# A one-core hybrid decoder layer: which projection runs beside the SSD, and how many attention heads run beside the SSD's output projection

## The chip, the cores and the metric

The kernel runs on one core of one Trainium2 chip. The metric is the device time of one execution in microseconds (us); the median of three runs is shown. PE is TensorE (matmuls; PEld its weight loads), DVE is VectorE, ACT is ScalarE, POOL is GpSimd, SP is SyncE.

## The reference

One decoder layer over 1024 tokens of width 1024, in float32:

- a mixer: one input projection of the normed input feeds an SSD (a chunked state-space scan, 8 chunks of 128 tokens, 8 heads) and a stick-breaking attention of 8 heads of width 64; both outputs are normed, joined and projected by `w_out`;
- a cross-attention to 256 memory tokens: 4 heads of width 128, with keys and values projected from the normed memory by `w_xk` and `w_xv`;
- an MLP with squared ReLU, 1024 to 4096 and back, and a final norm.

```
y_all = concat([rmsnorm(ssd(...) * silu(z)), rmsnorm(stick_breaking_attention(q, k, v))])
h = x + y_all @ w_out
m = rmsnorm(mem, g_mem);  k = m @ w_xk;  v = m @ w_xv
h = h + softmax(q k^T / sqrt(128)) v @ w_o
h = h + relu(rmsnorm(h) @ w1)^2 @ w2
```

## The kernel before, in words

Every large product is made in three matmuls: each operand is split into a high and a low part (`split`, L170: ACT rounds the high part, DVE subtracts it), and `mm3` (L207 to L210) adds high x high, high x low and low x high. Weights come as pieces of 128 x 512 floats, 256 KB (`piece`, L187): one DMA from SP's queue into a staging buffer (tag `wst`, two buffers, and a third, `wst3`, while the input stage lives), then the split into `whi` and `wlo`, a ring of six each. Pieces carry an earlier priority than the code around them (`later(-EARLY)`).

The order of the work is made in two steps. First, generators write it down: each yields a cost, and `interleave` (L229) runs two of them so that their shares of the given totals advance together. Then a scheduler, which is part of the language, orders each engine's instructions by priority, and the priority is the place at which an instruction was written; one that is ready can go ahead of an earlier one that is not, within the buffers that are free.

The stages around the change are these:

- **SSD** (`ssd`, L513; 8 chunks), interleaved with the fillers of `early`: `proj_z1`, `proj_v(0)`, `proj_qk(0)`, and the first `NF` = 1 of the list `late`. Fillers use four PSUM buffers here (`mm_ps`).
- **Attention** (`attention`, L700), heads 0 to `NHA` - 1, interleaved with the rest of `late`. A head has four steps of cost 3/36, 7/36, 11/36 and 15/36. A step makes scores (`z`, PE), their sigmoid (ACT), a running product along the row (`stay`, the scan of L756 on DVE), transposes (`wT`, PE), a split (ACT, DVE), and products with the values (`ops`, PE). Queries, keys and values go through DRAM (`qd`, `kd`, `vd`): SP stores them, POOL loads them for each head. Fillers use three PSUM buffers here (`qk_ps`).
- **Output projection of the SSD** (`out_first`, L835; total 17.6: 16 blocks of 12 matmuls with 512 columns, tile `o`, and eight transposing steps of 0.2), interleaved with the heads from `NHA` on.
- **Output projection of the attention** (L923 on), which needs all heads: `yB` (the scaled and split heads), 16 blocks in `o`, and a row factor `ro` from the sum of squares `osum`, through `sps` (PE) and one power on POOL.

The fillers: `proj_qk(pr)` (L577) projects the queries and keys of heads 2 pr and 2 pr + 1 from four weight pieces; it yields 2.0 four times, for 24 matmuls of 512 columns each, and each block is split and stored in four (queries) or six (keys) DMAs. `proj_v(ch)` (L567) yields 1.0 eight times, for 24 matmuls of 256 columns. `mem_kv` (L603) reads four pieces of memory for the sums of squares (`msq`), then for values and keys each eight weight pieces and four pieces of memory's transpose (split with a scale, in halves), 96 matmuls of 512 columns in all; it yields 0.5 sixteen times, holds two PSUM tiles through eight steps, transposes the keys (`mkT`) and stores both (`kmd`, `vmd`) for the cross-attention.

What is needed when is said by `need` (L653): at the second step of a head, the next head of the same group may ask that the fillers have run up to a given sum, and `interleave` then writes fillers until it is reached. Head 0 asks for 6.

```
late = [("qk", 1), ("qk", 2), ("v", 1), ("qk", 3)]
late.insert(MP, ("mem", 0))
...
ends = {f: 8.0 * (n + 1) for n, f in enumerate(late)}
return max(ends.get(("qk", h // 2), 0.0), ends.get(("v", h // 4), 0.0), float(N0) if h == 0 else 0.0)
...
early += [filler(*f, mm_ps) for f in late[:NF]]
late = late[NF:]
interleave(chain(*early), ssd(), SF - ZB + 8.0 * NF, 8.0)
...
interleave(chain(*[filler(*f, qk_ps) for f in late]),
           attention(range(0, NHA), bufA, need), 8.0 * len(late), float(NHA))
...
interleave(out_first(), attention(range(NHA, 8), bufA), 17.6, 8.0 - NHA)
```

Of the kernel before, what the change touches and what calls it, by code (L numbers as in the profile page):

```python
# [41 lines left out]
XSC = 0  # L42
SPP = 0
BPP = 0
MP = 4
OB = 1
KKB = 6

# [20 lines left out]
LAG = 1  # L69
OW = 1  # L70
NC = 6
NHA = 7
SJ = 0
EV = 100
GIVE = 0
# [16 lines left out]
def hybrid_trunk(ctx: ExitStack, tc: tile.TileContext, xT, x, cols, rows, gain, fing, wzd, wp, out):  # L92
# [136 lines left out]
    def interleave(a, b, total_a, total_b, need=None):  # L229


        da = db = 0.0
        a, b = iter(a), iter(b)
        live_a = live_b = True
        while live_a or live_b:
            if live_a and (not live_b or da / total_a <= db / total_b):
                v = next(a, None)
                live_a = v is not None
                da += v or 0.0
                continue  # L240
            v = next(b, None)
            if v is None:
                live_b = False
            elif isinstance(v, tuple):
                while live_a and da < v[1]:
                    w = next(a, None)
                    live_a = w is not None
                    da += w or 0.0
            else:
                db += v  # L250
# [391 lines left out]
    def chain(*gens):  # L642
        for g in gens:
            yield from g

    early = [z1_g, proj_v(0, sg_, mm_ps), proj_qk(0, sg_, mm_ps)]
    late = [("qk", 1), ("qk", 2), ("v", 1), ("qk", 3)]
    late.insert(MP, ("mem", 0))

    def filler(kind, i, ps_fn):  # L650
        return mem_kv(sg_, ps_fn) if kind == "mem" else (proj_qk if kind == "qk" else proj_v)(i, sg_, ps_fn)
# [153 lines left out]
    def qk_ps(name):  # L805
        return psum("m0", 4 - OB, name)

    interleave(chain(*[filler(*f, qk_ps) for f in late]),
               attention(range(0, NHA), bufA, need), 8.0 * len(late), float(NHA))
    third.clear()  # L810
# [24 lines left out]
    def out_first():  # L835
        def turned(th):
            for i in range(4):
                t4 = qk_ps("yT4")
                for j in range(4):
                    nc.tensor.transpose(out=t4[:, j * P:(j + 1) * P], in_=ytok[:, 4 * th + j, i * P:(i + 1) * P],  # L840
                                        identity=ident)
                yh, yl = yS[th][:, 0, i, :], yS[th][:, 1, i, :]
                act(yh, t4, scale=col(C_GSSD + i))
                stt(yl, t4, col(C_GSSD + i), yh.bitcast(F32), ALU.mult, ALU.subtract)
                yield 0.2

        first_ = turned(0)
        yield next(first_)
        for t in range(HD):
            load_h(0, t, yS[0][:, 0, 0, 0:1].bitcast(F32))  # L850
        yield from first_
        second = turned(1)
        for n in range(2):
            ws = pieces("wos", 4 * n, 4)
            for t in range(NT):
                ps = qk_ps("o1")
                with later(GIVE):
                    out_mm(ps, yS, ws, t)
                ns = slice(512 * n, 512 * n + 512)
                stt(h[t][:, ns], ps, ry[:, t:t + 1], h[t][:, ns], ALU.mult, ALU.add)  # L860
                if HL and 8 * n + t + HD < 16:
                    load_h((8 * n + t + HD) // 8, (t + HD) % 8, h[t][:, 512 * n:512 * n + 1])
                yield 1.0
                v = next(second, None)
                if v is not None:
                    yield v
# [6 lines left out]

    interleave(out_first(), attention(range(NHA, 8), bufA), 17.6, 8.0 - NHA)
    bctx.close()
# [592 lines left out]
```

## Time and profile before

| | |
|---|---|
| median of three runs | 1355.25 us (1353.1 to 1356.51) |
| the profiled execution | 1353.6 us, span 1351.9 us |
| busy share of the span | PE 97%, PEld 79%, DVE 70%, ACT 52%, POOL 15% |
| mean granted clock of PE | 0.997 |

By the first and last matmuls of the fillers' tiles, the stages lie so in the span: third filler of the SSD's stage, `qk` 0, from 172.8; `qk` 1 from 203.4 and `qk` 2 from 233.1, with the first head's scores from 249.8; the second values to 337; `qk` 3 to 387.7; memory 391.6 to 454; the SSD's output projection 459 to 522.4, with the last head's last products at 508; the attention's output projection to 574.2. The cross-attention and the MLP take the rest. The stretches in the rows below are cut there. Busy time is a union of an engine's instructions; a matmul's end is modelled.

### The profile page before, as it was taken

Reading aid. Unit: us, or ns where it says so; the run is one execution under the profiler, and the core shown is the slowest. Engines: PE = TensorE matmul, PEld = TensorE weight load, DVE = VectorE, ACT = ScalarE, POOL = GpSimd, SP = SyncE. Lnnn points to the kernel's source line nnn. Section 1 sums busy time; section 2 is a strip of 40 time slices with the busy share of each in tenths; the row PEclk is TensorE's granted clock in tenths of the full one; section 3 lists DMA queues with packets and bytes.
Section 4 is the critical chain, followed back from the end, with each engine's and each line's share of the span. In section 5 each row is a group of like instructions: output and inputs, shape, how many; then the busy total and the mean of one; then the engine's idle time right before and its main releaser. Section 6 shows DMA issues by size and latency. Waiting matters only on the chain.

```text
span 1351.9 us, 18376 instructions
## 1 busy us (share of the span) xinstructions
PE 1304.6 (97%) x6469; PEld 1062.8 (79%) x6469; DVE 949.1 (70%) x1527; ACT 700.8 (52%) x1341; POOL 199.6 (15%) x228
## 2 busy tenths in 40 slices
PE   8999999999988999999998999999999999999997
PEld 6989877788766778887876888888887787888885
DVE  7757865686789856545579766766667866589685
ACT  7454543565557633575445445544553595444453
POOL 0000000310211001022443323313330000000000
PEclk9999999999999999999999999999999999999999
DMA  6121345942556434121133554345449943633351
GB/s 220 40 64 48 101 133 130 266 131 73 150 151 207 149 88 130 32 64 32 32 141 131 180 164 153 133 151 164 140 154 337 312 130 94 236 95 97 95 156 70
DMA packets 95852, 181.68 MB, mean 134 GB/s; under 512 B 9808, under 2 KB 14992, under 8 KB 95760
## 3 DMA queue, kind: packets, MB, share of 16 engines
q1 hardware_dynamic: 85040, 155.78, 36.5%
q0 software_dynamic: 8624, 18.88, 5.1%
q10 hardware_dynamic: 2096, 5.84, 1.2%
q8 instruction: 51, 0.84, 0.3%
q14 instruction: 41, 0.34, 0.1%
HBM read 128.00 MB, written 52.46 MB: 133 GB/s over the span
## 4 chain that ended last, share of the span: by engine, by line
PE 82%; DVE 9%; ACT 3%; DMA 3%; issue 2%; POOL 1%; SPq 0%; POOLq 0%; ACTq 0%; DVEq 0%
PE P L210 7%; PE P L208 7%; PE P L209 7%; PE pr L208 7%; PE pr L209 7%; PE pr L210 7%; DVE stay L756 4%; PE ops L787 2%; PE o L210 2%; PE o L208 2%; PE o L209 2%; PE qkps L208 2%; PE qkps L210 2%; PE qkps L209 2%; PE wT L773 2%
## 5 line engine op out<-in xcount | busy, mean ns | idle before, releaser
L208 PE MATMUL pr<-whi 128*128 128x512 f32 x448 | 175.9, 396 | 2.9 <-ACT whi L107 2.9
L209 PE MATMUL pr<-wlo,whi 128*128 128x512 f32 x448 | 176.8, 395 | 0.0
L210 PE MATMUL pr<-whi,wlo 128*128 128x512 f32 x448 | 176.2, 393 | 0.0
L110 POOL TENSOR_TENSOR c<-c 128x512 f32<-128x512 f32 x60 | 87.0, 1460 | 201.4 <-ACT c L107 199.1
L110 DVE TENSOR_TENSOR wlo<-w1r,whi 128x512 fp32r<-128x512 f32 x92 | 81.7, 890 | 40.2 <-ACT whi L107 40.2
L107 ACT ACTIVATE whi<-w1r 128x512 fp32r<-128x512 f32 x92 | 57.8, 631 | 94.2 <-DVE w1r L110 48.7
L208 PEld LDWEIGHTS pr<-whi 128*128 128x128 f32 x448 | 83.9, 188 | 24.3 <-ACT whi L107 3.7
L210 PE MATMUL P<-T,wlo 128*128 128x512 f32 x256 | 100.9, 394 | 1.2 <-DVE wlo L110 1.2
L208 PE MATMUL P<-T,whi 128*128 128x512 f32 x256 | 100.8, 394 | 0.0
L209 PE MATMUL P<-T,whi 128*128 128x512 f32 x256 | 100.7, 394 | 0.0
L210 PEld LDWEIGHTS pr<-whi,wlo 128*128 128x128 f32 x448 | 84.1, 188 | 20.3
L209 PEld LDWEIGHTS pr<-wlo,whi 128*128 128x128 f32 x448 | 84.2, 188 | 19.8 <-DVE wlo L110 0.6
L107 ACT ACTIVATE c<-c 128x512 f32<-128x512 f32 x132 | 81.5, 628 | 25.8 <-DVE c L110 24.2
L107 ACT ACTIVATE whi<-wst 128x512 fp32r<-128x512 f32 (+1 forms) x88 | 54.5, 629 | 71.8 <-PE o L210 24.8
L756 DVE TENSOR_TENSOR_SCAN stay<-stay,dg 128x128 f32<-128x128 f32 (+3 forms) x64 | 85.3, 1347 | 9.2 <-ACT stay L107 9.1
L107 ACT ACTIVATE whi<-us 128x512 fp32r<-128x512 f32 x64 | 40.3, 630 | 78.7 <-PE pr L209 66.8
L110 DVE TENSOR_TENSOR wlo<-wst,whi 128x512 fp32r<-128x512 f32 (+1 forms) x88 | 61.6, 714 | 26.7 <-ACT whi L107 23.8
L209 PE MATMUL P<-B,whi 128*128 128x512 f32 x192 | 76.3, 397 | 0.0
L208 PE MATMUL P<-B,whi 128*128 128x512 f32 x192 | 76.2, 397 | 0.0
L210 PE MATMUL P<-B,wlo 128*128 128x512 f32 x192 | 76.0, 396 | 0.0
L110 DVE TENSOR_TENSOR wlo<-us,whi 128x512 fp32r<-128x512 f32 x64 | 44.8, 700 | 32.4 <-ACT whi L107 31.7
L110 DVE TENSOR_TENSOR wlo<-pair,whi 128x512 fp32r<-128x512 f32 x96 | 65.6, 684 | 0.0
(340 smaller groups left out, 3389.1 us busy)
## 6 DMA issues: line engine op xcount, KB each, us to landing
ud<-c SPq DMA_DIRECT2D x112, 256.0 KB, 3.4
wst<-in_wp SPq DMA_DIRECT2D x104, 256.0 KB, 2.7
w1r<-in_wp SPq DMA_DIRECT2D x16, 1024.0 KB, 6.4
us<-ud SPq DMA_DIRECT2D x64, 256.0 KB, 2.7
pair<-in_wp SPq DMA_DIRECT2D x16, 1024.0 KB, 7.6
kk<-kd POOLq DMA_DIRECT2D x32, 256.0 KB, 5.0
p<-ud SPq DMA_DIRECT2D x24, 256.0 KB, 2.7
u<-ud SPq DMA_DIRECT2D x24, 256.0 KB, 2.7
```

The lines of the kernel that those rows point to most:

```text
L107: nc.scalar.activation(out=out, in_=in_, func=func, **kw)
L110: (eng or nc.vector).tensor_tensor(out=out, in0=a, in1=b, op=op)
L208: nc.tensor.matmul(out=ps, lhsT=a[0], rhs=b[0], start=start, stop=False)
L209: nc.tensor.matmul(out=ps, lhsT=a[0], rhs=b[1], start=False, stop=False)
L210: nc.tensor.matmul(out=ps, lhsT=a[1], rhs=b[0], start=False, stop=stop)
L756: nc.vector.tensor_tensor_scan(out=stay[:, 0:W][:, ::-1], data0=stay[:, 0:W][:, ::-1], data1=B.dg1[:, S - W:S][:, ::-1], initial=0.0, op0= ...
L773: nc.tensor.transpose(out=t4[:, o:o + P], in_=wb[ii][:, b * P:(b + 1) * P], identity=ident)
L787: nc.tensor.matmul(out=ops[:, oc:oc + 256], lhsT=v, rhs=w[:, sb * 256:sb * 256 + 256], start=(s2_ == 0 and sb == 0 and j == 0), stop=(last ...
```

## The change

Two constants. `MP` is where memory's projection stands in the list of fillers; with 0 it stands first, so it is the one that `NF` takes into the SSD's stage, and second queries and keys go to the attention's fillers in its stead. `NHA` is how many heads run beside those fillers; the other heads run beside the SSD's output projection.

```
-MP = 4
+MP = 0
...
-NHA = 7
+NHA = 6
```

The lists, before and after: beside the SSD `z1`, `v` 0, `qk` 0 and `qk` 1 before, `z1`, `v` 0, `qk` 0 and memory after; in the attention `qk` 2, `v` 1, `qk` 3, memory before, `qk` 1, `qk` 2, `v` 1, `qk` 3 after. No operation is added or removed.

## Rows read from the trace of the kernel before

**Rows 1.** The profile's page: span, then busy us, share, instructions.

```profile
span 1351.9 us, 18376 instructions
...
PE 1304.6 (97%) x6469; PEld 1062.8 (79%) x6469; DVE 949.1 (70%) x1527; ACT 700.8 (52%) x1341; POOL 199.6 (15%) x228
```

**Rows 2.** Busy us (instructions) by stretch: from:to, length, engines, clock, DMA share, GB/s.

```profile
203.20:233.00 29.80, 29.80 (x144) 23.23 (x143) 17.01 (x31) 9.55 (x21) 0.00 (x0) 1.00 0.51 126
...
260.00:308.00 48.00, 44.08 (x300) 37.86 (x299) 42.17 (x61) 31.47 (x72) 8.95 (x14) 1.00 0.47 136
308.00:338.00 30.00, 27.76 (x203) 24.73 (x203) 19.31 (x30) 15.73 (x35) 2.71 (x5) 1.00 0.28 82
338.00:391.60 53.60, 48.73 (x261) 36.87 (x260) 40.23 (x58) 29.51 (x64) 12.48 (x17) 1.00 0.57 159
391.60:453.80 62.20, 54.87 (x307) 42.44 (x306) 57.52 (x92) 45.00 (x96) 5.54 (x9) 1.00 0.57 167
453.80:509.00 55.20, 51.59 (x270) 40.47 (x269) 35.42 (x51) 22.19 (x45) 3.22 (x15) 1.00 0.39 117
509.00:522.40 13.40, 13.40 (x59) 10.81 (x58) 13.30 (x19) 10.12 (x14) 2.65 (x5) 1.00 0.85 235
```

**Rows 3.** Timeline of PE inside a filler: start us, us, instruction.

```profile
240.06 0.39 PE L208 MATMUL qkps<-xh,whi 128*128 128x512 f32 x1
240.29 0.40 PE L209 MATMUL qkps<-xl,whi 128*128 128x512 f32 x1
```

**Rows 4.** Timeline: the second v projection's first matmul; head 0's last scan.

```profile
265.38 0.28 PE L208 MATMUL vps<-whi,xh 128*128 128x256 f32 x1
...
268.11 2.29 DVE L756 TENSOR_TENSOR_SCAN stay<-stay,dg 128x1024 f32<-128x1024 f32 x1 [0.43 <-ACT stay L107]
```

**Rows 5.** DVE groups, 203.2 to 233, beside the SSD's last chunks.

```profile
L110 DVE TENSOR_TENSOR ql<-qkps,qh 128x512 fp32r<-128x512 f32 x4 | 2.7, 686 | 2.3 <-ACT qh L107 2.3
...
L110 DVE TENSOR_TENSOR qkps<-qkps,rbc 128x512 f32<-128x512 f32 x2 | 1.4, 700 | 4.3 <-PE qkps L210 4.3
```

**Rows 6.** Tile kk, the attention's key loads, 32 of 256 KB.

```profile
DMA to landing us min/median/max: 2.7/5.0/9.2
```

**Rows 7.** DVE groups, 391.6 to 453.8, beside memory's projection.

```profile
L110 DVE TENSOR_TENSOR wlo<-wst,whi 128x512 fp32r<-128x512 f32 x17 | 11.0, 678 | 0.1
...
L117 DVE SCALAR_TENSOR_TENSOR wlo<-wst,colt,whi 128x256 fp32r<-128x256 f32 x12 | 5.2, 476 | 1.8 <-ACT whi L107 1.8
```

**Rows 8.** Timeline: a load, the split of what it brought, the next load.

```profile
403.88 0.33 SPq L191 DMA_DIRECT2D wst<-in_wp  x1
...
408.18 0.68 DVE L110 TENSOR_TENSOR wlo<-wst,whi 128x512 fp32r<-128x512 f32 x1
...
408.89 0.33 SPq L191 DMA_DIRECT2D wst<-in_wp  x1
```

**Rows 9.** DVE's scans, 453.8 to 509: count, busy us, mean ns, idle before.

```profile
L756 DVE TENSOR_TENSOR_SCAN stay<-stay,dg 128x128 f32<-128x128 f32 (+7 forms) x8 | 10.5, 1341 | 0.6 <-ACT stay L107 0.6
```

**Rows 10.** Timeline, end of the attention and start of the next projection.

```profile
510.31 2.08 DVE L117 SCALAR_TENSOR_TENSOR yB<-oT,colt,yB 128x512 fp32r<-128x512 f32 x3
...
520.65 1.21 DVE L110 TENSOR_TENSOR osum<-osum,osq 128x1024 f32<-128x1024 f32 x1
...
528.09 0.39 PE L934 MATMUL sps<-ones,osum 128*128 128x1 f32 x3
...
531.93 2.07 DVE L117 SCALAR_TENSOR_TENSOR h<-o,ro,h 128x512 f32<-128x512 f32 x3 [1.80 <-POOL ro L226]
```

**Rows 11.** Timeline of PE around a pause in the MLP's operand stage.

```profile
715.90 1.12 PE L256 MATMUL hT<-ident,hn 128*128 128x128 f32 x4 [3.98 <-POOL hn L110]
...
717.67 0.63 PE L208 MATMUL P<-B,whi 128*128 128x512 f32 x1
718.10 0.63 PE L209 MATMUL P<-B,whi 128*128 128x512 f32 x1
```

**Rows 12.** Busy time by stretch around that pause.

```profile
709.50:719.50 10.00, 6.02 (x22) 4.68 (x21) 9.84 (x14) 4.34 (x8) 6.58 (x5) 0.83 0.30 88
```

## The prediction

> **What bounds the kernel now.** I read the page's first lines, then busy time by stretch, then timelines at the places that the change touches. TensorE (PE) is shown busy for 97% of the span [rows 1]. Another order of work can therefore win only what PE idles, and the table of stretches shows where that is [rows 2]. Beside the last SSD chunks (203.2 to 233) PE is never idle. From 260 to 509, the attention, it is idle for 3.9, 2.2, 4.9, 7.3 and 3.6 us in the five stretches, 22 us together: 8.2, 7.5, 9.1, 11.8 and 6.5% of them. The worst is 391.6 to 453.8, where memory is projected beside heads 5 and 6, and there VectorE (DVE) is busy for 57.5 of 62.2 us, 92%. The best is 453.8 to 509, one head beside the SSD's output projection. Behind the attention PE is full again. The true loss is somewhat larger than the idle time: a matmul is shown for 0.39 us while the next starts 0.23 us later [rows 3], so a short gap hides in its tail. What binds in the attention is thus not one engine but PE and DVE close together, and the change moves DVE work between two stages.
>
> **What the two numbers do to the order.** Count a filler in its own units: a unit is 12 matmuls of 512 columns (24 of 256), 12 x 0.23 = 2.8 us of PE [rows 3]. Memory's projection has as many units (8) as second queries and keys, so PE's work does not change anywhere; it only moves. Worked out by the interleaving rule: before, heads 0 to 6 run beside 32 units (4.6 per head); after, heads 0 to 5 beside 32 (5.3 per head) and heads 6 and 7 share the 17.6 units of the output projection that head 7 had alone. Order of fillers after: second queries and keys, third, second values, fourth. Head 4 needs the second values; these now end at unit 24 instead of 16, so seven of their units (7 x 2.8 = 20 us of PE) are written in one piece ahead of head 3's second step, where before one was. After them 1.5 heads are written with no filler. I cost this at nothing, because the written order is only a priority: the second values' first matmul ran at 265.4, before head 0's last scan at 268.1 [rows 4], though it is written behind the last step of head 1. Fillers that are ready move ahead into idle PE time. If that cover is missing, those 1.5 heads run at the attention's own pace.
>
> Second queries and keys must now reach DRAM before head 2's loads. The last of their units is written before head 1's second step, so 33/36 of head 1 lies between. Eight heads share some 250 us, 31 each; the first are quicker, and two thirds of the mean is still 20 us. A projected block needs about 12 us from its last matmul to a loaded key (0.7 us scaling, 1.3 splitting, some 3 for six stores, 2 to land, 5.0 to load [rows 5, 6]). It stays hidden; if head 1 were quicker than that, DVE would wait for the difference.
>
> **The SSD stage pays.** Memory brings 16 weight pieces (split lo on DVE 0.678 us each), 8 of its own pieces in 16 halves (0.476), four evacuations of about 0.7: 10.8 + 7.6 + 2.9 = 21.3 us of DVE [rows 5, 7]. Second queries and keys take away four pieces, four splits of 0.686 and two scalings of 0.70: 2.7 + 2.7 + 1.4 = 6.8 [rows 5, 7]. DVE had 17.0 us in 203.2 to 233 [rows 2]; it gets 17.0 - 6.8 + 21.3 = 31.5, less two or three pieces that the ring of six lets it split ahead, some 29.5. At the fullest share that any stretch shows, 92%, this needs 32 us where the stretch has 29.8: +2.2. The pieces themselves: a staging buffer was loaded at 403.88, its content was split at 408.18, and the next load into a buffer was issued at 408.89 [rows 8], 5.0 us per turn, 1.7 us a piece with three buffers. With six pieces held when memory begins, 18 x 1.7 = 30 us: about the stretch, +0. As the upper bound, 23 pieces took the whole 62.2 us of the old stretch, 2.7 each, 18 x 2.7 - 29.8 = +19; but there they waited for matmuls that the attention's order held back, so I stay near the low end: **+2.5**. On the queues, SyncE's issues 28 loads and 8 stores in place of 4 loads and 20 stores: about equal time at 0.33 us a load [rows 8] and half a microsecond a store. GpSimd does nothing in that stretch [rows 2], so memory's one power there is free. ScalarE gets about as much more as DVE, some 15 us, where it had 9.6 [rows 2]; behind its splits wait the decay loads, which are issued a chunk ahead. The two accumulators of memory hold two of four PSUM buffers where one was in use: no more than a wait for evacuations of 0.7 us.
>
> **The attention gains.** 14.5 us of DVE work and about as much of ScalarE's leave a stage where each head's scans alone take 10.5 us of DVE [rows 9]. Not less than 0, since PE was idle at 9.1% in the neighbouring stretch with DVE only 75% busy; at most all 7.3 us of idle time in memory's stretch. At the neighbour's share 62.2 x (11.8% - 9.1%) = 1.7, at the best stretch's 3.3: **-2.5**. What binds next is the chain score, sigmoid, scan, transpose, split, product of each head. Two heads beside the output projection are in this term: 27 us of PE for the second one come where idleness was lowest.
>
> **The hand-over behind the attention pays.** When the last head was done at 509, 59 matmuls of the old projection, five units, 13.4 us, were still to do, and PE ran them without a gap [rows 2]. They covered what must follow on the heads' output: of the four scaled and split blocks that its first products need, three were ready by 512.4 and the fourth near 513.7; the sum of squares was ready at 521.9, and the factor used at 531.9, 3.8 us behind the row sums' start on PE at 528.1 [rows 10]. By the interleaving, seven units were written behind the last step and two of them had run by 509; after the change three are written there, so one, 2.8 us, remains. PE then has 2.8 us of it until 511.8, a gap of 1.9 to 513.7, four new units (11.2 us) into its four PSUM buffers, and somewhere among them a wait for the sum of squares. Cover lost wholly: 531.9 - 509 - 2.8 - 11.2 = +9; nothing lost: 0. Most of the chain can move up with DVE less crowded, so **+3.5**.
>
> A pause of PE costs more than itself here: after 3.98 us without work at 715.9, matmuls of 512 columns start 0.43 us apart, not 0.23 [rows 11], that is at 1.2 GHz in place of 2.4, and the granted clock over those 10 us is 0.83 [rows 12], a loss of 1.7. The sum holds none of this, since the pauses in it are 1.9 us and the like. The Trainium skill, "TensorE: Matmul & The Clock Gate", on how oscillation bites in real kernels, says that idle gaps of the array drop it to the lower rate, and that such a cost recurs with every gap. By that rule, with this row's price, the sum would be 1.7 us higher for each pause as long as this one.
>
> **Sum.** 2.5 - 2.5 + 3.5 = +3.5 on the profiled execution's own 1353.6 us: 1357.1. The median of the runs shown is 1.65 above that execution, so a median might read 1358.8. About 0.3% (4.1 us) is what a measurement of this kernel can tell from no change.
>
> **Rivals.**
> *DVE was the bound (faster).* If memory's splits starved the whole attention, its idle time falls to the best stretch's 6.5% of 249 us, 16.2 of 22, -5.8, and the two costs come near their low ends, +0.5: 1348. For it: 92% DVE in the worst stretch. Against it: 9.1% idle where DVE was 75% busy.
>
> *Head 6 starts late (slower).* The order asks for a filler's end only for a next head of the same group. Head 6 now opens a group, and its keys come from the last filler, written behind head 5's last step; before, memory's 8 units lay between. If that block is not pulled ahead by the 12 us worked out above, DVE waits while PE runs four units of output projection, and those lack beside head 7. Twelve us of attention without filler cost between nothing and all of it, I take the middle, 6, and the hand-over loses its last unit, 2.8: 3.5 + 8.8 = +12, 1366. It decides from a block that ends less than 12 us ahead of head 5's end. Against it: ready fillers run ahead [rows 4].
>
> *Half clock (slower).* Pauses as long as the one at 715.9 in the stream of pieces and at the hand-over: 2 x 1.7 more, and the two pauses 3 beyond the sum: 1363.5. The Trainium skill's rule above, in "TensorE: Matmul & The Clock Gate", names the same mechanism, and the trace agrees with it at 715.9.
>
> **How the numbers follow.** Near no change 0.37, faster 0.28, head 6 late 0.31, half clock 0.04; the predicted time is the first one's, 1357.1, whose own range is 1351 to 1359.5. The whole range takes in the middle of both sides: 1345 to 1368, leaving out a deeper gain and the far ends of the stream's and hand-over's bounds. Faster 0.28, same 0.37, slower 0.35.
>
> **What would show it.** Right: beside the last chunks DVE over 85% and PE idle for some 2 us; no stretch of the attention with DVE over 90% and PE idle above 10%; PE idle for 2 to 5 us around the first blocks of the attention's own projection. Wrong: PE full beside the last chunks and a shorter attention (then the relief was under-sized); a gap in the scans between heads 5 and 6, or long runs of plain attention behind the second values (then order decided, not load).

## The result, and the profile after

Nine executions of each kernel, taken in turns on one chip, gave 1364.94 us for the changed one (1360.25 to 1375.17) and 1355.25 us for the one before (1351.85 to 1357.14). The ratio is 1.0076, with a 95% interval of 1.0062 to 1.0091: slower by 0.76%, 9.7 us. That lies inside the forecast range, above the range of the likeliest case, and on the side to which the forecast gave 0.35.

The first profiled execution of the changed kernel (span 1373.5 us) was the slowest of the nine, 10 us above their median, with a granted clock of 0.985; for the reading a second profile of the same kernel is used, whose 1363.79 us is close to the median. The first lines of its page (they answer to [rows 1]):

```profile
span 1362.1 us, 18351 instructions
PE 1310.0 (96%) x6469; PEld 1062.3 (78%) x6469; DVE 947.8 (70%) x1527; ACT 702.1 (52%) x1341; POOL 197.5 (15%) x228
```

PE does the same 6469 matmuls as before, and the span is 10.2 us longer than the 1351.9 of [rows 1]. Where the time went is seen once the span is cut at the same events in both kernels. Below is the busy time by stretch of that second profile (columns as in [rows 2]): memory beside the SSD; five stretches of the attention; the 3.1 us between the last head and the next projection; and that projection's difficult middle.

```profile
203.50:238.40 34.90, 32.29 (x143) 22.22 (x141) 26.71 (x52) 20.92 (x45) 3.02 (x5) 1.00 0.68 205
260.00:308.00 48.00, 43.43 (x246) 33.60 (x247) 43.15 (x62) 30.02 (x65) 9.00 (x14) 1.00 0.58 157
308.00:344.00 36.00, 33.39 (x193) 26.04 (x191) 26.66 (x40) 19.37 (x42) 2.66 (x5) 1.00 0.56 142
344.00:383.00 39.00, 37.38 (x262) 32.58 (x261) 18.62 (x24) 16.89 (x36) 4.50 (x7) 1.00 0.37 107
383.00:440.00 57.00, 52.65 (x309) 41.63 (x308) 48.83 (x74) 34.68 (x74) 9.03 (x15) 1.00 0.41 114
440.00:521.00 81.00, 77.00 (x407) 59.31 (x406) 56.81 (x81) 33.52 (x70) 6.55 (x20) 1.00 0.33 96
521.00:524.10 3.10, 3.10 (x15) 2.50 (x14) 2.45 (x4) 3.00 (x6) 2.29 (x3) 1.00 0.14 27
...
538.90:552.00 13.10, 10.20 (x37) 8.69 (x38) 3.64 (x6) 0.00 (x0) 1.68 (x1) 0.61 0.00 0
```

The last line is the one to stop at: clock 0.61, and no work at all on ACT. The bookkeeping against the kernel before, each stretch from the first matmul of one stage to the first of the next:

| stretch | before, us | after, us | difference | predicted |
|---|---|---|---|---|
| fourth filler beside the SSD, to the first matmul of the next filler | 203.4 to 233.1 | 203.5 to 240.2 | +7.0 | +2.5 |
| attention with its fillers and the SSD's output projection | 233.1 to 522.5 | 240.2 to 524.1 | -5.5 | -2.5 |
| attention's output projection, first to last matmul | 522.5 to 574.1 | 524.1 to 585.9 | +10.2 | +3.5 |
| all behind it | 777.7 | 776.2 | -1.5 | 0 |

All three terms of the sum have the right sign, and all three are two to three times too small. The last 1.5 us are no larger than what separates two executions of one kernel; since each column is one execution, sums of such differences are good to about 2 us.

**The hand-over.** The timeline of the second profile from the last head on (it answers to [rows 10]):

```profile
520.75 0.28 PE L787 MATMUL ops<-wlast,vl 128*128 128x256 f32 x1
...
522.93 1.14 ACT L107 ACTIVATE whi<-wst 128x512 fp32r<-128x512 f32 x2
523.98 3.17 ACT L107 ACTIVATE yB<-oT,colt 128x512 fp32r<-128x512 f32 x5
530.56 0.63 ACT L107 ACTIVATE whi<-wst 128x512 fp32r<-128x512 f32 x1 [3.42 <-DMA wst<-in_wp]
...
531.71 0.62 ACT L107 ACTIVATE whi<-wst 128x512 fp32r<-128x512 f32 x1
532.23 1.05 ACT L107 ACTIVATE osum<-oT 128x1024 f32<-128x1024 f32 x1
...
534.96 3.87 DVE L110 TENSOR_TENSOR osum<-osum,osq 128x1024 f32<-128x1024 f32 x3
...
538.89 2.95 PE L934 MATMUL sps<-ones,osum 128*128 128x1 f32 x16 [3.41 <-DVE osum L110]
...
543.84 2.72 DVE L117 SCALAR_TENSOR_TENSOR h<-o,ro,h 128x512 f32<-128x512 f32 x4 [1.80 <-POOL ro L226]
544.74 0.77 PE L208 MATMUL o<-whi,yB 128*128 128x512 f32 x1 [2.90 <-DVE h L117]
```

And the same events of the kernel before, as far as [rows 10] does not show them:

```profile
507.98 0.28 PE L787 MATMUL ops<-wlast,vl 128*128 128x256 f32 x1
...
513.83 1.05 ACT L107 ACTIVATE osum<-oT 128x1024 f32<-128x1024 f32 x1
...
520.63 1.34 ACT L107 ACTIVATE whi<-wst 128x512 fp32r<-128x512 f32 x2 [1.38 <-PE o L210]
```

The last head's last products are done at 521.0 (508.3 before), and 14 matmuls of the old projection are left, where 62 were: one block of 12 and a bit. PE finishes them at 524.1, runs four blocks of the new projection into its four PSUM buffers without a gap, and then stands for 3.41 us until the sum of squares is there and for another 2.90 until the first buffers are emptied by means of the factor. Meanwhile ACT, which makes the squares, stands 3.42 us at a weight piece that has not landed, with the squares behind it in its queue; before, the squares ran ahead of the weight splits. The matmul at 544.74 takes 0.77 us, and its followers start 0.43 us apart, not 0.23: 1.2 GHz.

**Beside the SSD.** The waits of the staging tile `wst`, 203 to 239, second profile; the indented lines give us and times:

```profile
L107 ACT ACTIVATE whi<-wst x15: 613/631/632, 205.3 to 238.6; 128x512 fp32r<-128x512 f32 x15
...
  DMA wst<-in_wp: 13.4, 13
  ACT whi L107: 6.3, 7
```

Thirteen times, 13.4 us in all, the split of a piece (the last of them already the next filler's) waited for its DMA. DVE is busy for 26.71 of 34.90 us, 77%: it is not what binds here.

### The profile page after: what moved, and what is told of

Same layout as the page of the kernel before. It is cut to its first block, busy times and chain, and to the rows that moved or that the text cites. A ratio compares the mean times of both kernels' runs of the same rounds, so it can differ in the third digit from the quotient of the medians.

```text
span 1373.5 us, 18351 instructions
## 1 busy us (share of the span) xinstructions
PE 1317.3 (96%) x6469; PEld 1067.6 (78%) x6469; DVE 952.6 (69%) x1527; ACT 701.1 (51%) x1341; POOL 196.3 (14%) x228
## 4 chain that ended last, share of the span: by engine, by line
PE 59%; DVE 4%; DMA 1%; ACT 1%; issue 1%; POOL 0%; ACTq 0%; POOLq 0%; DVEq 0%
PE P L208 7%; PE P L210 7%; PE P L209 7%; PE pr L208 7%; PE pr L209 7%; PE pr L210 7%; PE o L210 2%; PE o L208 2%; PE o L209 2%; DVE stay L756 1%; PE ops L787 1%; PE xqps L208 1%; PE xqps L209 1%; PE xqps L210 1%; PE xops L210 1%
## 5 line engine op out<-in xcount | busy, mean ns | idle before, releaser
L756 DVE TENSOR_TENSOR_SCAN stay<-stay,dg 128x128 f32<-128x128 f32 (+3 forms) x64 | 85.4, 1349 | 10.5 <-ACT stay L107 10.2
L107 ACT ACTIVATE stay<-z,rq 128x512 f32<-128x512 f32 (+2 forms) x96 | 52.5, 581 | 29.3 <-PE z L753 17.1
```

The costliest lines, as they stand in the source:

```text
L107: nc.scalar.activation(out=out, in_=in_, func=func, **kw)
L756: nc.vector.tensor_tensor_scan(out=stay[:, 0:W][:, ::-1], data0=stay[:, 0:W][:, ::-1], data1=B.dg1[:, S - W:S][:, ::-1], initial=0.0, op0= ...
```

## The experiments

Three theories stood at the start: the hand-over lost its cover; the order of the heads (head 6's keys late) cost the time; the stream of pieces beside the SSD did. All ratios below are against the kernel before, in turns on the same chip; runs of different batches are best compared by them, since the kernel before itself read 1354.07 to 1355.78 us.

**The same kernel again.** No edit.

> The changed kernel once more, for a second profile, since its first profiled execution (1375.17 us) was 10 us above its median. If the pauses are a property of the order of work, memory's stretch beside the SSD again ends some 8 us late against the kernel before (next filler's first matmul near 242 instead of 233.1), and PE again pauses for several us behind the fourth block of the attention's own projection; only the half-clock stretches may differ in number and place, and the time should lie near 1364. If the pauses were an accident of that execution, one of the two is gone and the time is nearer 1358.

Measured: 1363.79 us in one execution, the second profile above. The long half-clock stretches at 227.7, 265.3 and 1070.8 of the first profile are gone; the one at the hand-over is there again (10.2 us from 539.6, 13.7 in the first). So that one belongs to the kernel, the others to the execution.

**Memory alone.** Seven heads beside the fillers, as before.

```
-NHA = 6
+NHA = 7
```

> Memory beside the SSD, but seven heads beside the other fillers as before. Load theory (memory's pieces stream too slowly beside the SSD, and the hand-over lacks cover): the SSD's stretch loses the same 8 us, the hand-over keeps its five covering blocks and loses nothing, the attention gains 2 to 4: 1355 + 4 to 6 = 1359 to 1361. Order theory (the fillers' new order starves the attention: seven blocks of second values in one piece, then heads without filler): here the order is more uneven still, since the fourth queries and keys are also written in one piece and two heads have no filler at all, so this is slower than the whole change, over 1366.

Measured: 1354.86 us, ratio 0.9999 (0.9989 to 1.0009). Moving memory's projection costs nothing and wins nothing. Both theories had expected more: 1359 to 1361, and over 1366. In its profile the stretch beside the SSD is 6.5 us longer than before and the attention 3.2 us shorter; the profiled execution of the kernel before was itself some 2 us under its median. Its stretches, beside the SSD and then from the last head on:

```profile
203.10:239.30 36.20, 32.86 (x150) 22.99 (x149) 27.72 (x53) 22.70 (x49) 4.84 (x8) 1.00 0.70 206
512.00:525.50 13.50, 13.50 (x60) 10.91 (x59) 13.39 (x19) 10.08 (x14) 2.61 (x5) 1.00 0.82 233
525.50:577.20 51.70, 51.70 (x260) 43.00 (x259) 25.55 (x41) 19.32 (x38) 1.68 (x1) 1.00 0.15 41
```

The hand-over is full again, as in [rows 2]'s last line: PE never idle, clock 1.00.

**Heads alone.** Memory where it was, six heads beside the fillers.

```
-MP = 0
+MP = 4
```

> Six heads beside the fillers and two beside the SSD's output projection, memory last in the attention as before. Load theory: nothing is lost beside the SSD, and the hand-over has only about one covering block left and pauses as in the changed kernel, so about 1355 + 5 to 10 = 1360 to 1365. Order theory: head 6's keys are written long before head 6 (memory's projection lies between), so nothing is late and the time is 1353 to 1357.

Measured: 1367.16 us, 1.0088 (1.0071 to 1.0106): the whole loss, and more than the 1360 to 1365 that was expected. Fourteen matmuls are left behind the last head, as in the changed kernel, and the wait is the same:

```profile
531.84 0.63 ACT L107 ACTIVATE whi<-wst 128x512 fp32r<-128x512 f32 x1 [3.60 <-DMA wst<-in_wp]
...
540.17 3.57 PE L934 MATMUL sps<-ones,osum 128*128 128x1 f32 x16 [3.56 <-DVE osum L110]
```

Here memory's units lie between head 6's keys and head 6, so the order that the rival "head 6 starts late" blamed is not in this kernel. It is as slow without it.

**Blocks kept back.** The changed kernel, with the total that `interleave` is told for the output projection lowered, so that the last blocks are written behind the last head.

```
-    interleave(out_first(), attention(range(NHA, 8), bufA), 17.6, 8.0 - NHA)
+    interleave(out_first(), attention(range(NHA, 8), bufA), 13.0, 8.0 - NHA)
```

> The whole change, but the share by which the output projection advances beside heads 6 and 7 is set so (total 13.0 instead of 17.6) that seven of its blocks are written behind the last head's last step, as in the kernel before, instead of three. Load theory: the pause behind the fourth block of the next projection goes, with its half clock: 6 to 10 us less than the whole change, 1355 to 1359. Order theory: the hand-over does not matter, the time stays within 2 us of 1365, or rises since heads 6 and 7 have less beside them.

Measured: 1356.57 us, 1.0006 (0.9995 to 1.0018). 62 matmuls are left behind the last head, and the loss is gone, with memory and the heads still in the changed order. Its timeline:

```profile
519.60 1.05 ACT L107 ACTIVATE osum<-oT 128x1024 f32<-128x1024 f32 x1
...
526.46 1.34 ACT L107 ACTIVATE whi<-wst 128x512 fp32r<-128x512 f32 x2 [1.43 <-PE o L210]
...
533.92 1.84 PE L934 MATMUL sps<-ones,osum 128*128 128x1 f32 x16
```

Two things differ from the changed kernel. The row sums start without a wait, and take 1.84 us, not 2.95. And the squares run ahead of the weight splits: the splits at 526.46 wait for PE to give back a buffer of the ring. With the old blocks unfinished, their weights still hold the ring of six, so the new splits come late in ACT's order. With the old blocks done, the new weights move up, and the squares stand behind them.

**The pause filled.** The changed kernel, with 16 matmuls ahead of the row sums and 14 behind them that compute nothing that is used (`OW` puts the row sums behind the fourth block, where PE ran them anyway). The pause keeps its length, but PE does not idle in it.

```
-OW = 1
+OW = 3
...
+                def warmer(n):
+                    for _ in range(n):
+                        nc.tensor.matmul(out=hot, lhsT=yB[0][:, 0, 3, 0:P], rhs=yB[0][:, 0, 3, :],
+                                         start=True, stop=True)
+
+                warmer(16)
...
+                warmer(14)
```

> The whole change with the pause at the hand-over filled by spare matmuls (16 ahead of the row sums, 14 behind them, 0.23 us each, their result unused); the order of the blocks stays. The wait itself is as long as before, so this prices the half clock alone. If the half clock that follows the pause (10.2 us at 1.2 GHz in the second profile of the change) costs anything, PE stays at 2.4 GHz there and the time falls by 3 to 5 us, to 1360 to 1362. If the blocks behind the pause are held by something else anyway (the factor, the evacuations), the time stays at 1364 to 1366.

Measured: 1362.02 us, 1.0061 (1.0047 to 1.0074). Its timeline and its stretches around the place:

```profile
537.78 3.84 PE L936 MATMUL hot<-yB 128*128 128x512 f32 x16
...
541.46 1.91 PE L941 MATMUL sps<-ones,osum 128*128 128x1 f32 x16
```

```profile
541.00:560.00 19.00, 19.00 (x92) 15.66 (x91) 7.64 (x12) 1.31 (x3) 1.68 (x1) 1.00 0.10 27
```

The clock is 1.00 where it was 0.61, the row sums take 1.91 us in place of 2.95, and the projection takes 58.6 us from first matmul to last where it took 61.8. So the half clock is worth some 3 us of the loss; the rest is the wait itself. These are one execution each. By the medians the gain is 2.9 us, by the ratios 2.0, and the ratios' intervals overlap.

**Sums first.** The changed kernel, with the squares given an earlier priority than the weight splits.

```
-    act(osum, oT[:, 0, :], AF.Square)
+    with later(-2 * EARLY):
+        act(osum, oT[:, 0, :], AF.Square)
...
```

> The whole change, but ScalarE squares the heads' output for the row factor ahead of the splits of the next weight pieces, instead of behind them. If the pause is long because ScalarE's queue stands at a weight piece that has not landed (3.75 us, with the squares behind it), the row sums come some 8 us earlier, the pause shrinks under 3 us and its half clock goes: 6 to 9 us less than the whole change, 1356 to 1359. If the chain behind the last head is long by itself, the squares only change places with the scaled blocks and less than 3 us is won: 1362 to 1365.

Measured: 1357.78 us, 1.0031 (1.0018 to 1.0043): 7 us less than the changed kernel by the medians, 6 by the ratios. Its timeline:

```profile
524.44 1.06 ACT L107 ACTIVATE osum<-oT 128x1024 f32<-128x1024 f32 x1 [0.90 <-PE ops L787]
...
527.30 1.14 ACT L107 ACTIVATE whi<-wst 128x512 fp32r<-128x512 f32 x2
...
533.52 1.21 DVE L110 TENSOR_TENSOR osum<-osum,osq 128x1024 f32<-128x1024 f32 x1
...
537.55 1.84 PE L935 MATMUL sps<-ones,osum 128*128 128x1 f32 x16
```

The first square starts 0.1 us after the last head's last product (524.35), and PE reaches the row sums with the sum ready. What is left of the wait is the start: the first yB block now waits 2.3 us for its split, since squares stand ahead of that. The control, the same edit in the kernel before:

> The kernel before with the squares ahead of the weight splits, a control for the sixth run. If the squares' place matters only where the covering blocks are gone, this is within 1 us of the kernel before, 1354 to 1356. If it shortens the chain behind the last head in any order, this is 3 us or more faster as well.

Measured: 1356.55 us, 1.0005 (0.9991 to 1.002). Where five blocks cover the chain, its order is worth nothing. So the edit repairs the changed kernel's hand-over and nothing else.

**Memory in one pass.** On "memory alone": values and keys are made together, so that memory's transpose is read and split once, 20 pieces in place of 24. Four PSUM tiles are held through the pass.

```
-        for key in ("mv", "mk"):
-            ps = [ps_fn("mkv") for _ in range(2)]
-            for k in range(KB):
-                if k % 2 == 0:
+        pss = {key: [ps_fn("mkv") for _ in range(2)] for key in ("mv", "mk")}
+        for k in range(KB):
+            if k % 2 == 0:
...
+            for key in ("mv", "mk"):
```

> Memory beside the SSD and seven heads (as in the second run), with memory's own transposed pieces loaded and split once for keys and values together: 20 pieces instead of 24, 4 us less of VectorE, four PSUM tiles held at once. Stream theory (pieces set the pace beside the SSD, 34 us for 22 us of matmuls): the stretch shortens by 4 x 1.4 to 1.7 us, 5 to 7, and the time is 1348 to 1351. Rival (VectorE with the SSD's own work, or the SSD's chain, sets the pace): within 2 us of the second run's 1354.9. Against it may go that four held PSUM tiles keep the next filler from starting, a loss of up to 5 us.

Measured: 1361.4 us, 1.0057 (1.0043 to 1.007), a miss for both theories. The stream did get shorter: memory's last product ends at 234.3, where it ended at 237.3. But PE then stands for 8.61 us, and no filler's matmul follows before 247.2:

```profile
241.45 0.69 DVE L720 TENSOR_TENSOR v<-v,v 128x512 f32<-128x512 f32 x1 [5.18 <-DMA v<-vd]
...
242.65 0.68 DVE L110 TENSOR_TENSOR ql<-mkT,qh 128x512 fp32r<-128x512 f32 x1
...
245.19 1.51 PE L756 MATMUL z<-kk,qs 128*128 128x256 f32 x4 [8.61 <-DMA vmd<-ql]
```

```profile
237.00:247.00 10.00, 1.81 (x7) 1.59 (x8) 3.98 (x8) 4.59 (x8) 3.10 (x6) 0.50 1.09 346
```

Four finished tiles must now leave PSUM together. Three do by 235.9, but the third is transposed into a new tile. Then DVE stands 5.18 us at head 0's values, which have not landed, with the split of that tile behind it in its queue, and the last of the four is copied only at 243.24. The DMA share of these 10 us is 1.09, and the granted clock 0.50. It may be that PE has no free tile until then, which is not shown; nor was it taken apart whether the four tiles or the late loads are the cause. Five staging buffers (below) show the same wait of DVE, 5.2 us, and there PE does not stop. With six heads and the lower total beside it:

> The whole change with seven blocks kept back for the hand-over (as in the fourth run) and memory in one pass. If both causes are settled by this (stream and hand-over), what is left is the attention's gain of 3 to 5 us and nothing is paid: 1348 to 1352, faster than the kernel before. If stream is not what held the SSD's stretch, it lies where the fourth run lay, 1356 to 1357.

Measured: 1364.77 us, 1.0074 (1.0061 to 1.0087), the same stop (DVE waits 5.5 us for head 0's values) and 3.4 us more. Neither says anything of the stream's price, so another test was needed.

**Five staging buffers.** On "memory alone", two more buffers for the pieces while memory is projected, five in place of three.

```
+        if fourth:
+            if nst_[0] % 5 == 0:
+                return third[0].tile([P, 528], F32, tag="wst3", bufs=1, name="wst")
+            if nst_[0] % 5 < 3:
+                return fourth[0].tile([P, 528], F32, tag="wst4", bufs=2, name="wst")
+            return wr.tile([P, 528], F32, tag="wst", bufs=2, name="wst")
```

> Memory beside the SSD and seven heads (as in the second run), with five staging buffers instead of three while memory is projected; the same loads, splits and matmuls. Stream theory (a load cannot be issued before a buffer has been split, 5 us per turn): memory's last matmul comes near 231 to 233 instead of 237.3, and the time falls by 3 to 5 us, to 1350 to 1352. Rival (ScalarE's and VectorE's split rate, or the DMA engines' own rate, sets the pace): memory ends at 236 or later and the time stays within 2 us of 1354.9.

Measured: 1349.38 us, 0.9953 (0.9937 to 0.997): 6 us faster than the kernel before, 5.5 than memory alone with three buffers. Memory's last product ends at 235.3, between the 231 to 233 of the stream theory and the 236 of its rival; the time decides for the first. The waits of the staging tile, 203 to 239, first of memory alone, then with five buffers, and the stretch to the next filler:

```profile
  DMA wst<-in_wp: 12.9, 13
```

```profile
  PE mkv L215: 4.3, 2
  DMA wst<-in_wp: 2.6, 4
...
  PE mkv L216: 2.4, 1
```

```profile
202.90:236.40 33.50, 31.38 (x150) 23.64 (x149) 28.27 (x53) 22.30 (x48) 0.00 (x0) 1.00 0.72 219
```

The waits for pieces fall from 12.9 us to 2.6, and what they gave way to is PE itself (4.3 and 2.4 us waiting for a place in the ring). The next filler starts 33.5 us after memory's first product, not 36.2. That is 2.7 of the 5.5 us; the fillers behind it run ahead by about as much again (fourth queries and keys begin at 363.0, not 368.4), which no run took apart.

**All three.** The changed kernel with the lower total, the sums first and five staging buffers.

> The whole change with its two losses treated: seven blocks kept back for the hand-over and the squares ahead of the weight splits (fourth and sixth run), and five staging buffers for memory. If hand-over and stream are the whole price of the change, the attention's gain of 3 to 5 us is left: 1349 to 1352, under the kernel before. If the stream is not shortened by buffers, 1354 to 1357.

Measured: 1349.51 us, 0.9954 (0.9936 to 0.9972). This beats both kernels as well, by as much as five buffers alone. With its hand-over repaired, a second head beside the output projection wins nothing.

## Why the prediction was right and where it was not

**The whole.** The measured median is 6.1 us above the 1358.8 that the prediction gave for a median. It lies in the range because the range was taken up to 1368 for rivals, not because the sum was near: against the second profile the three terms were off by +4.5, -3.0 and +6.7 us, and the second took back part of the others.

**What held.** The direction of each term, and the mechanism of two: the attention was relieved, and the hand-over lost its cover. Beside the SSD it was not DVE. That order costs nothing where fillers are ready early: the fourth queries and keys are written behind the third step of head 4, but their first matmul ran before head 3's last scan, and from 369 to 395 PE is busy for 24.24 of 26 us. (The fuller stretch from 344 to 369 is mostly the second values, which ran as the one piece that the order made of them.)

```profile
369.58 0.39 PE L208 MATMUL qkps<-xh,whi 128*128 128x512 f32 x1
...
380.27 2.29 DVE L756 TENSOR_TENSOR_SCAN stay<-stay,dg 128x1024 f32<-128x1024 f32 x1 [0.15 <-ACT stay L107]
```

No attention stretch has DVE over 90% with PE idle above 10%, as was to be seen. One block was to remain behind the last head, 2.8 us; 14 matmuls, 3.1 us, remained.

**The hand-over, predicted +3.5, measured +10.2.** Here the sum failed, at the sentence "Most of the chain can move up with DVE less crowded". Counted from the end of the last head's last product, the factor was used 531.9 - 508.3 = 23.6 us later before, and 543.84 - 521.0 = 22.8 us later after. It moved up by 0.8 us. DVE was indeed free, but the chain hung on ACT's queue, which the prediction did not look at. Before, the first square began 5.5 us after the last head, and the sum of squares was ready 13.6 us after it and then waited for PE to come to it; after, the first square began 11.2 us after it, and the sum was ready at 534.96 + 3.87 = 538.83, 17.8 us after. The slack was used up by the lost cover, and the chain grew by 4.2 us on top, for the squares now stood behind four weight splits and a wait of 3.42 us for a DMA. Sums first took away 6 to 7 us; the control shows that this is not a general gain. The predicted gap of 1.9 us ahead of the first yB block did not come; the wait stood wholly behind the fourth, 6.3 us of idle PE where 2 to 5 were to be seen.

**The half clock, predicted 0, measured about 3 of those 10.2.** The whole of it in the second profile:

```profile
539.60:549.85 10.25, 7.35 (x24) 6.24 (x24) 2.89 (x5) 0.00 (x0) 1.68 (x1) 0.50 0.00 0
```

The projection lost 3.41 + 2.90 = 6.3 us of idle time, and 10.2 us at 1.2 GHz, in 2.9 of which PE idled anyway: (10.2 - 2.9) / 2 = 3.7. Together 10.0, against 10.2 measured; filling the pause gave 3.2 back. The prediction priced such a stretch at 1.7 us and left it out, since it saw only a pause of 1.9 us coming. The pauses were 3.4 and 2.9, like the 3.98 of [rows 11], and the rival "half clock", given 0.04, was a real part of the loss. The Trainium skill, "TensorE: Matmul & The Clock Gate", in its section "HAM oscillation — how this bites in real kernels", tells of a kernel in which waits for DMA make each next tile's matmuls start at the lower clock, and counts that cost beside the waits themselves; the trace agrees, 6.3 us of idle and 3.7 us of slow matmuls. Had the hand-over's upper bound held this slow stretch, it would have been 9 + 3.7, near 13.

**Beside the SSD, predicted +2.5, measured +7.0.** The prediction asked DVE first: it was to do 29.5 us of work at 92%. It did 26.7 at 77%, where over 85% was to be seen; only PE's idle time, 2.6 us, was as foreseen. The price of the stream was right: 19 pieces were still to be split when memory's first product ran, and ACT began these splits between 205.29 and 235.78, 30.5 us over 18 steps, 1.7 us a piece, where the sum had 18 pieces at 1.7. In the second profile:

```profile
205.29 0.61 ACT L107 ACTIVATE whi<-wst 128x512 fp32r<-128x512 f32 x1
...
235.78 0.63 ACT L107 ACTIVATE whi<-wst 128x512 fp32r<-128x512 f32 x1 [0.52 <-DMA wst<-in_wp]
```

The step that failed is the one behind it, "about the stretch, +0": it took the stream for the whole stretch. The stream begins 1.8 us after memory's first product, and 4.4 us pass from its last split to the next filler's first matmul at 240.2, for the products of that piece, the keys' transposes, and the next filler's own pieces, which come last in the same stream. 1.8 + 30.5 + 4.4 = 36.7 us, 7.0 more than the 29.7 of before. With five buffers the same 19 splits begin between these:

```profile
204.84 0.62 ACT L107 ACTIVATE whi<-wst 128x512 fp32r<-128x512 f32 x1
...
227.64 0.63 ACT L107 ACTIVATE whi<-wst 128x512 fp32r<-128x512 f32 x1 [0.47 <-DMA wst<-in_wp]
```

That is 22.8 us, 1.3 a piece. So five buffers make the stream itself faster, and PE, idle for 2.1 of 33.5 us, no longer waits for a piece.

**The attention, predicted -2.5, measured -5.5 in the profile, -3.2 with memory alone.** The relief was real. PE's idle time from 260 to 521 is 17.2 of 261 us, 6.6%, against 22 of 249 before, 8.8%. Of the 5.5 a part is only borrowed: the blocks that ran inside the attention are those that the hand-over lacked. With them kept back the attention took 288.1 us, from 240.3 to 528.4, only 1.3 less than before. That is how moving a head between the two loops can come out at nothing.

**The rivals.** "DVE was the bound" named a true relief, but it was smaller than the cost beside the SSD until that stage had more buffers; with them, and with seven heads, the time, 1349.4, came near the 1348 that it gave. "Head 6 starts late" gave 1366, close to what was measured, for a reason that is not there. In the changed kernel heads 4, 5 and 6 begin their scans at 383.3, 410.2 and 440.7; between the starts of head 5's last scan and head 6's first lie 9.3 us, and it was 8.1 from head 4 to head 5. PE's waits from 440 to 470 sum to 1.7 us, none of them for keys, and blocks kept back has the same order at 1356.57. A time that fits is no evidence for its mechanism.

**What stays open.** What stopped PE with memory in one pass. Which part of the gain of five buffers is made beside the SSD and which in the attention. Whether the old order would gain from more staging in its own memory stretch was not tried: the two buffers lie in storage that ends with the SSD. Why some executions have further half-clock stretches, as the first profile had, is not known.

## What to carry to other kernels

Work that runs beside a stage's tail is its cover: before you use more of it earlier, count what is left behind the last dependent step, and follow the chain behind that through the order of work on every engine that it uses, for a faster finish lets other work (here weight splits waiting for a DMA) move up in front of it. A stage that gets more weight pieces can need more staging before it needs a faster engine: look at what its splits wait for, not at how busy VectorE is. Where two constants change together, run each alone; here one was free and the other was the whole loss.

## What the runs showed of the hardware that was not expected

A few idle microseconds cost about half as much again: pauses of 3.4 and 2.9 us at the hand-over came with a stretch of 10.2 us at 1.2 GHz in the second profile, in which even the 16 one-column products `sps` took 2.95 us in place of 1.84. Matmuls whose results nobody uses, put into the two pauses, kept the clock at 1.00 and shortened the projection by 3.2 us, one execution each. The length of such a stretch is not fixed by the kernel: nearly the same two pauses (3.73 and 2.90 us in the first profile) came with 13.7 us there (545.1 to 558.8) and 10.2 in the second.
